# Padded buffers, S5 tables on GpSimd's queue and a last FFN on the unnormed residual, in a two-layer hybrid trunk

## The chip, the cores and the metric

The kernel runs on one core of a Trainium2 chip. The metric is the device time of one execution in microseconds, as the median of several runs. A core has TensorE for matmuls, VectorE and ScalarE for elementwise work, GpSimd for odd work, and SyncE, which here only issues DMAs. ScalarE and GpSimd have a DMA queue of their own as well.

## The reference

It is a trunk of two layers over 256 latent tokens and 256 context tokens of width 1024. Each layer is a half SwiGLU step, a mixer and another half SwiGLU step; every sublayer norms its input, shifts and scales it, and adds a gated result to the residual.

```
def ffn_half_step(h, m, k, g, w_gate, w_up, w_down):
    shift, scale, gate = m[:, :, 3 * k], m[:, :, 3 * k + 1], m[:, :, 3 * k + 2]
    hn = modulate(rmsnorm(h, g), shift, scale)          # rmsnorm(h, g) * (1 + scale) + shift
    return h + 0.5 * gate * swiglu(hn, w_gate, w_up, w_down)
...
for i in range(DEPTH):                                  # DEPTH = 2
    lat = ffn_half_step(lat, m_lat, 0, norm_ffn1[i], *ffn1)
    cx = ffn_half_step(cx, m_ctx, 0, norm_ffn1[i], *ffn1)
    # even: latent attention heads and S5 channel groups; odd: Hyena channels and RG-LRU channels
    y_ctx, y_lat = even_mixer(...) if i % 2 == 0 else odd_mixer(...)
    lat = lat + m_lat[:, :, 5] * y_lat
    lat = ffn_half_step(lat, m_lat, 2, norm_ffn2[i], *ffn2)
    if not last: cx = the same for the context
return rmsnorm(lat, final_norm)
```

The FFN's hidden width is 2816. The attention has 8 heads, the S5 part 32 groups of 16 channels with 64 complex states, scanned in both directions. The context drops out behind the odd mixer, so the last FFN and the final norm see the latent half alone.

## The kernel before

Everything lies transposed: 128 channels on the partitions, 512 tokens in the columns (context 0 to 255, latent 256 to 511). The residual `res` is a constant tile of 8 x 512. Matmuls run in float32r with operands split into a high and a low part: `mm3` issues three matmuls for each block of 128 channels (lines 158, 159 and 160; with one stream order kept, all three stand on line 155). A weight block comes in by `wload`: a DMA from SyncE's queue into one of four `raw` buffers (line 142), a cast on ScalarE (148) and a subtraction on VectorE (149) into one of four `w` buffers.

A tile framework places instructions and buffers: each engine runs its own list in order, a pool gives a tag so many buffers, and a request for a buffer waits until its last user is done. The constant pool `cst` comes first in memory, then `rawp`, `wp`, the small tiles `sm`, and then the pools of a stage, which `phase` opens in the order of its arguments.

- In the first stage the FFN runs while `s5_prepare` builds tables for eight passes of S5 and writes them to DRAM: `d_mb`, `d_g`, `d_v`, `d_e`.
- In the even mixer, `s5_states` loads the tables `mb` and `et` of a pass (lines 916 and 918) and `s5_out` loads `gm` (958) and, in eight pieces, `tz` from `d_v` (962), all from SyncE's queue. VectorE does the scan between the two (935 to 950). The store of a pass's result to `d_y` goes out from GpSimd (971). The passes are interleaved with keys and queries of four pairs of heads and then with the eight heads: scores (L848 to L866), transposed probabilities (881, 887), values (900). Keys get their rotary part by a DMA from GpSimd (774). GpSimd also does two small memsets a pass (942, 949).
- Between the odd mixer and the last FFN, `out_proj` (through `down`) adds each of eight residual tiles (429) and its squares (291, 292); then `norm_proj` takes the row statistics (253 to 278), norms each tile (309, 314, 316) and starts the matmuls.
- `final` does the same at the end: statistics, row broadcast, a multiply for each of eight tiles (1266) and a store of each (1269). The host transposes the result.

## Time and profile before

| | |
|---|---|
| median of 3 runs | 1797.6 us (1797.04 to 1797.97) |
| the profiled execution, its own time | 1795.22 us |
| its span, from the first instruction to the last end | 1793.4 us |
| mean granted TensorE clock | 0.986 of full speed |

A profile is of one execution. A line of it names an engine, the kernel's line, the operation, and "written <- read" tiles with their shapes. Busy time is the union of an engine's instructions; TensorE's matmuls overlap in the pipeline, so the distance from one start to the next is the pace, and the duration of one is longer.

### The profile page before, as it was taken

The page shows a single profiled execution, that of the slowest core. Times are in us where ns is not written, and L with a number is a line of the kernel's source. Part 1 is how long each engine was busy: PE and PEld are TensorE (multiplying, and loading weights), DVE is VectorE, ACT ScalarE, POOL GpSimd, SP SyncE. Part 2 cuts the span into 40 slices and gives each one's busy share as a digit, 9 for nine tenths or more (in the row PEclk, how much of TensorE's full clock was granted, in tenths as well). Part 3 has the DMA queues.
Part 4 walks back from the last instruction along what each step waited for, and adds up shares of the span by engine and source line. Part 5 has one row for each costly group of instructions (what it writes and reads, how often), then busy time and mean ns, then how long its engine had stood idle before and what let it go on. Part 6 is the DMA issues. An engine that isn't in the chain of part 4 may idle for free.

```text
span 1793.4 us, 24725 instructions
## 1 busy us (share of the span) xinstructions
PE 1727.7 (96%) x9364; PEld 1444.7 (81%) x9364; DVE 1252.9 (70%) x2464; ACT 684.1 (38%) x1082; POOL 13.2 (1%) x47
## 2 busy tenths in 40 slices
PE   5999999999989999999999999999999999789997
PEld 3778777779868788778888888888888888589997
DVE  7999999987488668776666686544543576875555
ACT  4433333343445653222222233222122357554442
POOL 0000000000000000000000000000000000000000
PEclk9999999999998999999999999999999999799999
DMA  9566666652465453464454544555433225146552
GB/s 324 173 216 211 223 214 216 210 189 90 125 185 172 120 189 115 154 223 152 147 183 153 164 130 130 179 173 163 156 117 95 94 94 201 49 150 191 183 185 92
DMA packets 108055, 292.63 MB, mean 163 GB/s; under 512 B 21216, under 2 KB 36448, under 8 KB 107680
## 3 DMA queue, kind: packets, MB, share of 16 engines
q1 hardware_dynamic: 102368, 287.39, 49.8%
q10 hardware_dynamic: 4928, 2.10, 0.7%
q8 instruction: 73, 1.20, 0.3%
q0 software_dynamic: 640, 1.57, 0.3%
q14 instruction: 46, 0.38, 0.1%
HBM read 272.20 MB, written 18.28 MB: 162 GB/s over the span
## 4 chain that ended last, share of the span: by engine, by line
PE 87%; DVE 7%; DMA 2%; ACT 1%; issue 1%; SPq 1%; DVEq 0%; ACTq 0%
PE mm L158 25%; PE mm L160 25%; PE mm L159 25%; PE mm L155 6%; DVE w L149 1%; DMA h<-in_modw_dram 1%; PE mm L1148 1%; SPq L981 1%; DVE nt L309 1%; DMA x<-d_g 1%; DVE x L316 1%; DMA x<-d_v 0%; PE ps L278 0%; PE ps L631 0%; PE ps L1059 0%
## 5 line engine op out<-in xcount | busy, mean ns | idle before, releaser
L159 PE MATMUL mm<-x,w 128*128 128x512 f32 (+1 forms) x1600 | 575.1, 360 | 0.0
L160 PE MATMUL mm<-x,w 128*128 128x512 f32 (+1 forms) x1600 | 574.5, 360 | 0.0
L158 PE MATMUL mm<-x,w 128*128 128x512 f32 (+1 forms) x1600 | 569.4, 361 | 4.5 <-ACT x L314 3.3
L148 ACT CAST w<-raw 128x1024 fp32r<-128x1024 f32 (+2 forms) x324 | 328.5, 1018 | 527.7 <-issue 254.1
L149 DVE TENSOR_TENSOR w<-raw,w 128x1024 fp32r<-128x1024 f32 (+2 forms) x324 | 384.0, 1187 | 191.7 <-ACT w L148 190.8
L158 PEld LDWEIGHTS mm<-x,w 128*128 128x128 f32 x1600 | 300.9, 189 | 55.9 <-ACT x L314 3.9
L159 PEld LDWEIGHTS mm<-x,w 128*128 128x128 f32 x1600 | 301.8, 189 | 48.9 <-issue 2.0
L160 PEld LDWEIGHTS mm<-x,w 128*128 128x128 f32 x1600 | 301.8, 189 | 48.7 <-issue 1.2
L225 DVE CUSTOM_DVE_ANT_0 junk<-m,sc 128x1024 f32<-128x1024 f32 x224 | 273.3, 1220 | 1.8 <-DMA m<-in_modw_dram 0.2
L158 PE MATMUL mm<-h,w 128*128 128x512 f32 (+1 forms) x632 | 229.2, 367 | 0.0
L160 PE MATMUL mm<-h,w 128*128 128x512 f32 (+1 forms) x632 | 228.4, 364 | 0.0
L159 PE MATMUL mm<-h,w 128*128 128x512 f32 (+1 forms) x632 | 228.3, 363 | 0.0
L429 DVE SCALAR_TENSOR_TENSOR res<-mm,mraw,res 128x256 f32<-128x256 f32 x192 | 86.1, 480 | 103.7 <-PE mm L160 92.8
L459 DVE TENSOR_TENSOR h<-h,mm 128x512 f32<-128x512 f32 (+1 forms) x88 | 54.6, 621 | 128.5 <-PE mm L160 111.0
L458 ACT ACTIVATE h<-mm 128x512 f32<-128x512 f32 (+1 forms) x88 | 48.0, 545 | 234.5 <-PE mm L160 223.7
L159 PEld LDWEIGHTS mm<-h,w 128*128 128x128 f32 x632 | 119.1, 188 | 20.6 <-issue 1.0
L158 PEld LDWEIGHTS mm<-h,w 128*128 128x128 f32 x632 | 118.6, 188 | 21.0 <-issue 1.1
L160 PEld LDWEIGHTS mm<-h,w 128*128 128x128 f32 x632 | 118.9, 188 | 20.5 <-issue 0.6
L155 PE MATMUL mm<-x,w 128*128 128x256 f32 x384 | 66.1, 289 | 6.7 <-DVE x L316 6.2
L314 ACT ACTIVATE x<-nt,mraw 128x256 fp32r<-128x256 f32 x88 | 42.9, 506 | 54.5 <-DVE nt L309 54.5
L155 PEld LDWEIGHTS mm<-x,w 128*128 128x128 f32 x384 | 53.9, 188 | 11.6 <-DVE x L316 9.2
L165 DVE TENSOR_TENSOR h<-h,h 128x512 fp32r<-128x512 f32 (+1 forms) x88 | 54.5, 619 | 0.0
(345 smaller groups left out, 1604.5 us busy)
## 6 DMA issues: line engine op xcount, KB each, us to landing
raw<-in_wgu_dram SPq DMA_DIRECT2D x176, 512.0 KB, 3.8
m<-in_modw_dram SPq DMA_DIRECT2D x130, 512.0 KB, 4.3
raw<-in_wd_dram SPq DMA_DIRECT2D x64, 512.0 KB, 3.6
raw<-in_wd_dram SPq DMA_DIRECT2D x32, 384.0 KB, 3.3
raw<-in_od_in_dram SPq DMA_DIRECT2D x20, 512.0 KB, 3.5
h<-in_modw_dram SPq DMA_DIRECT2D x12, 512.0 KB, 9.9
raw<-in_ev_in_dram SPq DMA_DIRECT2D x10, 512.0 KB, 3.5
d_mb<-mbt SPq DMA_DIRECT2D x16, 256.0 KB, 2.9
```

What stands on the lines that cost most here:

```text
L148: nc.scalar.copy(hi[:, :n], raw[:, :n])
L149: nc.vector.tensor_sub(lo[:, :n], raw[:, :n], hi[:, :n])
L155: mm = lambda *a, **k: self.keep(self.nc.tensor.matmul(*a, **k))
L158: mm(ps, lhsT=wh, rhs=xh, start=first and i == 0, stop=False)
L159: mm(ps, lhsT=wh, rhs=xl, start=False, stop=False)
L160: r = mm(ps, lhsT=wl, rhs=xh, start=False, stop=last and i == n - 1)
L165: self.nc.vector.tensor_sub(lo, src, hi)
L225: nc.vector.tensor_tensor_reduce(self.junk, w, self.sc[:, v, :], 1.0, 0.0, ALU.mult, ALU.add, raw[:, dt, v : v + 1])
L314: self.last_act = nc.scalar.activation(x[:, 0, c0:c1], y, AF.Identity, bias=b)
L429: self.nc.vector.scalar_tensor_tensor(r, ps[:, c0:c1], gate[:, i, VEC[h] : VEC[h] + 1], r, op0=ALU.mult, op1=ALU.add)
L458: nc.scalar.activation(s[:, 0, lo:hi], pg[:, lo:hi], AF.Silu)
L459: nc.vector.tensor_mul(s[:, 1, lo:hi], s[:, 0, lo:hi], pu[:, lo:hi])
```

## The change

- Two pads of 136 and 64 float32 a partition are put at the head of the constant and the small pool, and the first stage's pools are opened in another order (`x`, `h`, then the rest).
- In the first stage the kernel writes a fifth table, `d_z`, from `d_v`: the shifted pieces that `tz` needs, laid out as one block, by four DMAs a pass from GpSimd.
- In the even mixer `mb`, `et`, `gm` and `tz` (now one DMA from `d_z`) are loaded from GpSimd's queue. GpSimd's memsets and the rotary key copies go to VectorE, the store to `d_y` to ScalarE's queue. The scores of the first head are emitted with the first pair's keys and queries.
- The last FFN (`ffn_last`) no longer norms its input. While the odd mixer's `out_proj` finishes a residual tile, `unscaled` writes it times gain into the high and low parts, and puts the shift into two further columns. The matmuls run over 258 columns; the row norm `rb` is multiplied onto gate and up behind the matmul and the shift's product is added as a bias.
- In the last `down`, `final_tiles` multiplies each finished tile by the final gain and transposes it into four PSUM buffers; `final` scales those by the row statistics and stores them row by row, so that the host need not transpose.

```
+        for p, k in ((self.cst, 136), (self.sm, 64)):
+            p.tile([P, k], F32, tag="pad", name=f"pad{k}", bufs=1)
+        self.done = None
...
         if last:
             self.stat(i, h)
+            if self.done is not None:
+                self.done(i, h)
...
+    def ffn_last(self, l, k, xs):
+        nc, t = self.nc, self.t
+        idx = 2 * l + k // 2
+        n = NTOK
+        with self.tc.high_priority(offset=SOON):
+            rb = self.slot("g", [P, n])
+            nc.scalar.copy(rb, self.rstd([self.acc[LAT]], self.inv_d))
+        gate = self.need(l, 3 * k + 2)
+        for f0, f1 in CHUNKS:
+            hid = []
+            for f in range(f0, f1):
+                pg, pu = self.pm(), self.pm()
+                for g, ps in enumerate((pg, pu)):
+                    w = self.wload(t["wgu"][idx, f, g], D)
+                    self.mm3(ps[:, : n + 2], self.wparts(w, KT), self.parts(xs, 0, n + 2))
+                b = self.small([P, 2], "bias")
+                s = self.slot("g", [P, 2, n])
+                nc.vector.tensor_copy(b[:, 0:1], pg[:, n : n + 1])
+                nc.vector.tensor_mul(s[:, 0, :], pg[:, :n], rb)
+                nc.scalar.activation(s[:, 0, :], s[:, 0, :], AF.Silu, bias=b[:, 0:1])
+                nc.vector.tensor_copy(b[:, 1:2], pu[:, n : n + 1])
+                nc.vector.tensor_mul(s[:, 1, :], pu[:, :n], rb)
+                nc.vector.scalar_tensor_tensor(s[:, 1, :], s[:, 1, :], b[:, 1:2], s[:, 0, :], op0=ALU.add, op1=ALU.mult)
+                hd = self.slot("x", [P, 2, T2], F32R)
+                self.split(hd[:, 0, n:T2], hd[:, 1, n:T2], s[:, 1, :])
+                hid.append(hd)
+            if f1 == NF:
+                self.done = self.final_tiles()
+            self.down(lambda i: t["wd"][idx, i][:, f0 * P : f1 * P], hid, gate, [LAT], f1 == NF, f1 - f0)
+
+    def unscaled(self, l, k, xs):
+        nc = self.nc
+        sh, sc = self.mod[l, 3 * k], self.mod[l, 3 * k + 1]
+        def done(i, h):
+            x, r, g = xs[i], self.res[:, i, h[0] : h[1]], sc[:, i, 0:1]
+            with self.tc.high_priority(offset=SOON):
+                nc.scalar.activation(x[:, 0, :NTOK], r, AF.Copy, scale=g)
+                nc.vector.scalar_tensor_tensor(x[:, 1, :NTOK], r, g, x[:, 0, :NTOK], op0=ALU.mult, op1=ALU.subtract)
+        for i, x in enumerate(xs):
+            self.split(x[:, 0, NTOK : NTOK + 2], x[:, 1, NTOK : NTOK + 2], sh[:, i, 0:1].to_broadcast([P, 2]))
+        return done
...
         nc.sync.dma_start(self.d_v[q], vt)
+        dv = self.d_v[q]
+        for g in range(4):
+            nc.gpsimd.dma_start(
+                self.d_z[q][:, g, :].rearrange("(r c) m -> r c m", r=L),
+                bass.AP(dv.tensor, dv.offset + g * 32 * 240, [[16, L], [240, 16], [1, P]]),
+            )
...
-                nc.gpsimd.dma_start(k[64:96, h, :], st["kr"][64:96])
+                nc.vector.tensor_copy(k[64:96, h, :], st["kr"][64:96])
...
+            if p == 0:
+                pr0 = self.scores(qs[0][:, 0, :], ks[0][:, 0, :])
...
-        nc.sync.dma_start(mb, self.d_mb[q])
+        nc.gpsimd.dma_start(mb, self.d_mb[q])
...
-        nc.sync.dma_start(et, self.d_e[q].rearrange("p e g c -> p e (g c)"))
+        nc.gpsimd.dma_start(et, self.d_e[q].rearrange("p e g c -> p e (g c)"))
...
-        nc.gpsimd.memset(rz[:, :, 0:1], 0.0)
+        nc.vector.memset(rz[:, :, 0:1], 0.0)
...
-        nc.gpsimd.memset(hv[:, :, 0:1], 0.0)
+        nc.vector.memset(hv[:, :, 0:1], 0.0)
...
-        nc.sync.dma_start(gm, self.d_g[q])
+        nc.gpsimd.dma_start(gm, self.d_g[q])
         tz = self.slot("x", [P, 4, P])
-        dv = self.d_v[q].rearrange("(g c) m -> c g m", g=4)[0:16]
-        for r in range(L):
-            nc.sync.dma_start(tz[r * 16 : (r + 1) * 16], dv[:, :, r * 16 : r * 16 + P])
+        nc.gpsimd.dma_start(tz, self.d_z[q])
...
-        nc.gpsimd.dma_start(d_y[q * 4 : (q + 1) * 4].rearrange("g s c n -> (s c) g n"), ys)
+        nc.scalar.dma_start(d_y[q * 4 : (q + 1) * 4].rearrange("g s c n -> (s c) g n"), ys)
...
+        self.xl = [self.slot("hy", [P, 2, T2], F32R) for _ in range(KT)]
+        self.done = self.unscaled(1, 2, self.xl)
         self.out_proj("od_out", 1, os, [LAT])
+        self.done = None
+
+    def final_tiles(self):
+        nc = self.nc
+        self.fin = [[self.pm() for _ in range(2)] for _ in range(2)]
+        def done(i, h):
+            y = self.slot("g", [P, NTOK])
+            nc.scalar.activation(y, self.res[:, i, h[0] : h[1]], AF.Copy, scale=self.gain[:, 6, i : i + 1])
+            for j in range(2):
+                nc.tensor.transpose(self.fin[j][i // 4][:, i % 4 * P : (i % 4 + 1) * P], y[:, j * P : (j + 1) * P], self.ident)
+        return done
 
     def final(self):
         nc = self.nc
-        self.rb[LAT] = self.rstd([self.acc[LAT]], self.inv_d)
-        for i in range(KT):
-            y = self.slot("h", [P, NTOK])
-            nc.vector.scalar_tensor_tensor(
-                y, self.res[:, i, NTOK:T2], self.gain[:, 6, i : i + 1], self.rb[LAT], op0=ALU.mult, op1=ALU.mult
-            )
-            nc.sync.dma_start(self.out[i], y)
+        _, r = self.rstd_stats([self.acc[LAT]], self.inv_d)
+        for j in range(2):
+            for q in range(2):
+                y = self.slot("g", [P, T2])
+                if q:
+                    nc.scalar.activation(y, self.fin[j][q], AF.Copy, scale=r[:, j : j + 1])
+                else:
+                    nc.vector.tensor_scalar(y, self.fin[j][q], r[:, j : j + 1], None, op0=ALU.mult)
+                (nc.scalar if q else nc.sync).dma_start(self.out[j, :, q * T2 : (q + 1) * T2], y)
...
-        self.phase(x=8, **s5p, gs=2, sc=1, junk=1, m=2, ct=1, h=10)
+        self.phase(x=8, h=10, sc=1, junk=1, m=2, **s5p, gs=2, ct=1)
...
-        self.phase(x=8, h=10)
-        self.ffn(1, 2, [LAT])
+        self.ffn_last(1, 2, self.xl)
         self.final()
```

## Rows read from the trace of the kernel before

**Rows 1.** The page's first part: busy time, share of the span, instructions.

```profile
PE 1727.7 (96%) x9364; PEld 1444.7 (81%) x9364; DVE 1252.9 (70%) x2464; ACT 684.1 (38%) x1082; POOL 13.2 (1%) x47
```

**Rows 2.** Windows by stage: stretch, length, PE PEld DVE ACT POOL, clock, DMA, GB/s.

```profile
62.00:404.00 342.00, 341.52 (x1591) 270.68 (x1592) 317.22 (x595) 128.06 (x199) 1.01 (x9) 1.00 0.66 208
404.00:500.00 96.00, 94.31 (x573) 83.35 (x572) 57.51 (x171) 36.65 (x63) 4.33 (x10) 1.00 0.42 116
500.00:610.00 110.00, 101.39 (x620) 82.40 (x619) 91.50 (x178) 63.36 (x154) 6.67 (x19) 0.92 0.55 167
...
630.00:1480.00 850.00, 844.94 (x4069) 696.98 (x4068) 524.61 (x901) 259.46 (x365) 0.00 (x0) 1.00 0.46 148
1480.00:1520.00 40.00, 40.00 (x281) 34.73 (x280) 24.43 (x37) 29.17 (x44) 0.00 (x0) 1.00 0.58 200
...
1591.00:1782.00 191.00, 189.71 (x1584) 189.51 (x1584) 111.19 (x154) 85.35 (x125) 0.00 (x0) 0.99 0.51 160
```

**Rows 3.** Windows of two dense stretches, of 512 and of 256 columns.

```profile
1200.00:1300.00 100.00, 100.00 (x432) 81.08 (x431) 51.22 (x73) 24.46 (x29) 0.00 (x0) 1.00 0.50 158
1640.00:1700.00 60.00, 60.00 (x508) 60.00 (x507) 35.07 (x45) 27.60 (x38) 0.00 (x0) 1.00 0.61 194
```

**Rows 4.** The chain of work, odd mixer's plain fp32 matmuls: start, length, what.

```profile
1476.73 12.88 PE mm L1148 x30
```

**Rows 5.** TensorE's waits: total us, times, longest.

```profile
PE ps L966 <- DMA x<-d_v: 7.3, 1, 7.3
```

**Rows 6.** Timeline of SyncE's queue in the even mixer: start, length, line, operation.

```profile
523.02 8.32 SPq L142 DMA_DIRECT2D raw<-in_ev_out_dram  x3
531.44 0.38 SPq L958 DMA_DIRECT2D x<-d_g  x1
```

**Rows 7.** The chain of work behind that issue.

```profile
531.44 5.08 DMA x<-d_g
```

**Rows 8.** Window behind TensorE's wait.

```profile
545.00:562.00 17.00, 17.00 (x112) 14.55 (x112) 11.79 (x22) 9.18 (x22) 1.54 (x4) 0.84 0.53 155
```

**Rows 9.** Timeline of GpSimd: key copies and one store of a pass.

```profile
467.05 2.14 POOL L774 DMA_DIRECT2D q<-kr  x4 [86.65 <-issue]
561.45 0.75 POOL L971 DMA_DIRECT2D d_y<-ys  x1 [4.46 <-ACT ys L970]
```

**Rows 10.** DMA issues, 470 to 625 us: count, KB each, median us to landing.

```profile
d_y<-ys POOLq DMA_DIRECT2D x8, 128.0 KB, 2.7
```

**Rows 11.** VectorE's groups by form: count, busy us, mean ns, idle before.

```profile
L833 DVE TENSOR_TENSOR q<-q,nt 32x256 f32<-32x256 f32 x8 | 3.2, 415 | 0.2
L668 DVE MEMSET et<- 128x8 f32 x8 | 0.5, 65 | 0.1
```

**Rows 12.** Timeline of TensorE between the odd mixer and the last FFN.

```profile
1583.59 0.28 PE L160 MATMUL mm<-x,w 128*128 128x256 f32 x1
1586.68 0.58 PE L253 MATMUL ps<-inv_d,acc 128*128 128x1 f32 x4 [2.82 <-DVE acc L292]
...
1591.62 0.80 PE L158 MATMUL mm<-x,w 128*128 128x256 f32 x2 [1.11 <-ACT x L314]
```

**Rows 13.** VectorE's groups by form from 1591 us to the end.

```profile
L149 DVE TENSOR_TENSOR w<-raw,w 128x1024 fp32r<-128x1024 f32 x56 | 68.3, 1225 | 45.9 <-ACT w L148 45.9
L429 DVE SCALAR_TENSOR_TENSOR res<-mm,mraw,res 128x256 f32<-128x256 f32 x24 | 11.3, 481 | 16.4 <-PE mm L160 16.2
L459 DVE TENSOR_TENSOR h<-h,mm 128x256 f32<-128x256 f32 x22 | 9.3, 421 | 11.3 <-PE mm L160 6.0 <-ACT h L458 5.0 <-issue 0.3
L267 DVE SCALAR_TENSOR_TENSOR rs_a<-rs_y,rs_v 128x1 f32<-128x1 f32 x6 | 1.0, 215 | 0.0
```

**Rows 14.** Timeline of the end.

```profile
1785.57 0.76 PE L278 MATMUL ps<-ident,rs_y 128*128 128x128 f32 x4 [2.02 <-DVE rs_y L269]
1786.36 3.22 DVE L1266 SCALAR_TENSOR_TENSOR h<-res,gain,ps 128x256 f32<-128x256 f32 x8 [0.73 <-PE ps L278]
1786.87 3.78 SPq L1269 DMA_DIRECT2D out_dram<-h  x8
```

More of the change, by code (lines that the diff above doesn't have):

```diff
@@ L687, in s5_prepare @@
         self.d_v = dt("d_v", [P, 240])
+        self.d_z = dt("d_z", [P, 4, P])
         self.d_e = dt("d_e", [P, 2, 8, 64])
@@ L810, in even_mixer @@
             i = s5_begin()
-            pr = self.scores(qs[h // 2][:, h % 2, :], ks[h // 2][:, h % 2, :]) if h < H else None
+            pr = None
+            if h < H:
+                pr = self.scores(qs[h // 2][:, h % 2, :], ks[h // 2][:, h % 2, :]) if h else pr0
             s5_end(i)
@@ L1486 @@
         aps[name] = nc.dram_tensor(f"in_{name}_dram", a.shape, mybir.dt.from_np(a.dtype), kind="ExternalInput").ap()
-    out = nc.dram_tensor("out_0_dram", (KT, P, NTOK), F32, kind="ExternalOutput").ap()
+    out = nc.dram_tensor("out_0_dram", (2, P, D), F32, kind="ExternalOutput").ap()
     with tile.TileContext(nc, schedule_with_timeline_sim=True) as tc:
@@ L1491 @@
     got = r.results[0]["out_0_dram"]
-    return np.ascontiguousarray(got.reshape(D, NTOK).T).reshape(1, NTOK, D)
+    return np.ascontiguousarray(got).reshape(1, NTOK, D)
```

## The prediction

> **What bounds the kernel now.** I read first the busy table, then the span cut into stages with each engine's busy time, then the chain of work, the waits of TensorE, and last SyncE's and GpSimd's own queues in the even mixer. TensorE is busy 96% of the span, VectorE 70% [rows 1], but the stages differ [rows 2]: from 62 to 404 us TensorE is full and VectorE has 317 of 342 us; from 630 to 1480 and from 1591 to 1782 TensorE is full and VectorE has room; from 500 to 610 neither is full (TensorE 101, VectorE 91.5 of 110). So what counts is the pace of TensorE's stream nearly everywhere, and waits in a few places.
>
> The pace is worth a second look. In a dense 100 us there are 432 matmuls of 512 columns, 231.5 ns each, and in a dense 60 us 508 of 256 columns, 118.1 ns each [rows 3], at a granted clock of 1.00, the 2.4 GHz level. That is 556 and 283 cycles: the difference is 273 cycles for 256 columns, 1.066 a column, with about 10 cycles per instruction. The plain fp32 matmuls of the odd mixer (30 in 12.88 us [rows 4]) take 429.3 ns, 1030 cycles for 512 columns: 2 cycles a column and 6 over. They read at half the rate of the float32r ones and lose nothing. So the float32r stream loses some 7% to something that bites only at full reading rate.
>
> **The padding.** The pads add 544 bytes a partition behind the constants and 256 behind the small tiles; the new bias tile adds 4 x 32. Adding up the tiles of the kernel before (constants step in 32 bytes) the raw buffers begin at byte 37,344, the weights at 53,728, x at 97,376: each 32 bytes past a multiple of 64, and so all large buffers, h of the first stage among them. Afterwards raw begins at 37,888, the weights at 54,272 and x at 98,304, all multiples of 1,024, and h follows x directly because the first stage's pools change order. No float32r operand before lies on a multiple of 64, so no row shows that pace; it has to be bounded. From below the gain is nothing: the loss belongs to the float32r stream whatever its address. From above the whole loss goes: the fp32 rows' 6 cycles over give (512+6)/2.4 = 216 ns and 109 ns. A supposition with the right size can be made: if each piece of 64 bytes (16 columns) that straddles a boundary costs one cycle more, 512 columns take 544+6 cycles = 229 ns and 256 take 278 = 116 ns, within 3 ns of both measured paces, and it would stay hidden at half rate as in [rows 4]. Two shapes and the fp32 rows fit it, so I take the value near the upper end: 217 and 111 ns, a cut of 6.3% and 6.0%.
>
> [...]
>
> By stage [rows 2]: 62 to 404: 6.3% of 342 is 21.5 us, but TensorE would then need 320 us against VectorE's 317, so I take 15. 404 to 500: 5. 630 to 1480: 6.3% of 845 = 53. 1480 to 1520: 2. 1591 to 1782: 6.0% of 190 = 11. From 500 to 630 and 1520 to 1591, where VectorE or transfers set the pace, nothing. Sum 86 us.
>
> **The even mixer.** TensorE's longest wait of the stage is 7.3 us for the d_v table [rows 5]. It is no slow transfer: SyncE stood 8.32 us on ev_out weight loads whose buffers were not free, and only behind them issued d_g and the eight small d_v loads [rows 6]; d_g then landed in 5.08 us [rows 7]. Behind the hole the granted clock is 0.84 in the mean from 545 to 562 [rows 8], part of it at the 1.2 GHz level after TensorE had stood idle, worth at most 0.16 x 17 = 2.7 us. With all four tables on GpSimd's queue no weight load stands ahead of them, and d_z makes eight issues into one. The order on that queue is mb, et of a pass, then gm, tz of the pass before; each still waits for a free x buffer. GpSimd now carries one d_y store a pass, 0.75 us, and eight key copies, 0.53 us each [rows 9]; its memsets and these go away, so four loads of perhaps 0.75 to 1 us a pass come to 3 or 4 us of the 12 us that a pass takes (nine turns in the 110 us of [rows 2]). Its stores land in 2.7 us [rows 10]. The d_y store goes to ScalarE, behind the copy that makes it, and adds an issue there. The 32 d_z writes run in the first stage, where GpSimd does nothing else.
>
> The floor is VectorE: 91.5 us busy of 110 [rows 2]. It takes on eight key copies of 32x512 (0.4 each from the 32x256 row, 0.8 at most) and 16 memsets of 0.065 [rows 11], 4 to 7.5 us, about half of it before 500 where it has 38 us free [rows 2]; the first head's scores move ahead as well. So 110 can come down to about 97: between 3 and 16, I take 11 us saved.
>
> **The last FFN's entry.** The last od_out matmul starts at 1583.59; then come the sum of squares, the row statistics at 1586.68, and the first matmul of the new FFN at 1591.62 [rows 12], 8 us in which TensorE does nothing but the statistics' small matmuls. Now each finished residual tile is scaled by ScalarE and split by VectorE at once, and the norm is applied behind the matmul; seven of eight operands wait ready, and the eighth takes residual, copy and split, about three times 0.48 us [rows 13], under the first 21 matmuls, 2.5 us. Saved 7 to 9, I take 8. Cost: VectorE gets one more 128x256 split (0.48) per od_out tile, near its limit there; per hidden tile it has two multiplies, a scalar_tensor_tensor and a split (0.42, 0.42, 0.48, 0.42) and two one-column copies (0.2 at most) where it had a multiply and a split, 1.3 us more by [rows 13]. With two weight splits of 1.23 that is 4.6 us beside the 5.7 us of 48 matmuls: covered. 258 columns instead of 256 on 1,056 matmuls: 2/2.4 ns each, +1 us.
>
> **The end.** Before, row broadcast, eight multiplies of 3.22 us and eight stores issued from 1786.87 over 3.78 us [rows 14]. Now gains and 16 transposes run inside the down stream (at most 0.19 us each by the four of L278, up to 3 us; I take 2), and behind the statistics two scaled copies on each of two engines (0.5 to 1 us each) and two stores on each of two queues: the end comes 3 to 4 us earlier. Net 1 to 2 us saved; four of the six PSUM buffers are then held, and two remain for down, whose residual takes 0.48 us of a tile's 24 matmuls, 2.8 us. I take 2.
>
> **Sum.** 86 + 11 + 8 - 1 + 2 = 106. The profiled execution took 1795.2 us (span 1793.4 and 1.8 around it), 2.4 under the median of 1797.6. 1795.2 - 106 = 1689, on the median's scale 1691; I say 1690.
>
> **Rivals.** *The padding does nothing* (0.30). The loss per column belongs to float32r at full rate; the same 1.066 holds for x, h and q tiles, which speaks for neither. The remaining 20 us come alone: 1778, from 1768 to 1788. The Trainium skill (SBUF — State Buffer, "Door 1: The DMA port swizzle") counts 16-byte lines, of which a start 32 bytes on crosses no more, and this rival follows from it; its "Operand start alignment" says that it timed nothing. No row here decides.
>
> *No change to be measured* (0.04): the padding is idle, and VectorE's extra work in the mixer and at the od_out tail takes back the 20 us: 1797.
>
> *GpSimd's queue becomes the bound* (0.07): its four loads a pass take so long to issue that a pass waits for them. A pass takes some 12 us, so it decides from 3 us a load. At 4 us, 16 us a pass, eight passes lose 32 us; with an idle padding and the 9 us of the last FFN and end: 1797.6 + 32 - 9 = 1821. Against it stand 0.75 us an issue and 2.7 us to landing in a stretch where VectorE is over 80% busy [rows 9, 10]. The Trainium skill (SBUF — State Buffer, "SBUF: two separate sides", the box on SWDGE) has VectorE's two-port operations lock GpSimd out of writing descriptors; these rows show no such delay so far.
>
> *Padding pays, the rest as said* (0.59): 1690, its own range 1670 to 1712 (all of the loss and a VectorE that keeps up in the first stage, or half of the first stage's and no gain in the mixer).
>
> The 80% range takes in the first and the last of these: 1670 to 1786. By 0.2% either side (3.6 us, about what a measurement of this kernel tells from no change): faster 0.89, same 0.04, slower 0.07.
>
> **What would show it.** Dense stretches of float32r matmuls at 216 to 218 ns and 110 to 111 ns; if they stay at 231 and 118 the padding is idle and the time is near 1778. No wait of TensorE on d_v or d_z above 2 us, and GpSimd issues under 1 us. No gap above 1 us between od_out and the last FFN, and an end within 4 us of the last statistics. VectorE above 95% from 62 to 404 us would show that the first stage gave less than 15.

## The result and the profile after

The kernel after takes 1775.8 us (median of 4 runs, 1775.09 to 1776.01), the kernel before beside it 1797.3 (1796.6 to 1797.97): ratio 0.988, 95% interval 0.9863 to 0.9897. The change makes the kernel 21.5 us faster, where 1690 us and a cut of 106 were forecast. The time lies inside the range, close to the rival in which the padding does nothing (1778), but not for that rival's reason: a change of pace by itself gave 22 us (e6), and the rest of the change nothing on balance.

The first part of the page after: busy time, share of the span (1773.2 us), instructions, as in [rows 1].

```profile
PE 1708.4 (96%) x9376; PEld 1444.4 (81%) x9376; DVE 1271.4 (72%) x2570; ACT 696.5 (39%) x1103; POOL 37.4 (2%) x79
```

Windows of the kernel after by stage, columns as in [rows 2]:

```profile
62.00:396.00 334.00, 333.29 (x1586) 269.17 (x1587) 314.67 (x593) 126.55 (x198) 19.79 (x39) 1.00 0.70 220
396.00:500.00 104.00, 98.27 (x584) 87.43 (x583) 60.64 (x178) 39.53 (x67) 2.71 (x5) 0.97 0.36 116
500.00:610.00 110.00, 101.18 (x626) 79.52 (x624) 94.32 (x200) 66.52 (x158) 14.54 (x27) 0.95 0.49 158
630.00:1460.00 830.00, 824.99 (x4055) 692.42 (x4054) 520.89 (x898) 256.31 (x360) 0.00 (x0) 1.00 0.47 151
1460.00:1500.00 40.00, 40.00 (x279) 34.61 (x278) 24.33 (x37) 29.09 (x44) 0.00 (x0) 1.00 0.60 198
1564.00:1764.00 200.00, 195.91 (x1611) 194.85 (x1609) 132.59 (x248) 91.69 (x129) 0.00 (x0) 0.99 0.51 161
```

The stretch from 630 us, 850 us long before, now takes 830; that from 500 still takes 110, with TensorE as busy as before. The last FFN, from its first matmul to its last residual tile, takes 9 us more than before, and TensorE, full before, misses 4 us in it.

The two dense stretches, to be held against [rows 3]:

```profile
1200.00:1300.00 100.00, 100.00 (x443) 82.81 (x442) 52.65 (x76) 23.97 (x28) 0.00 (x0) 1.00 0.52 165
1640.00:1700.00 60.00, 60.00 (x502) 60.00 (x501) 40.57 (x69) 27.23 (x34) 0.00 (x0) 1.00 0.58 182
```

At 512 columns 443 matmuls fit into 100 us: 225.7 ns where there were 231.5, and not 217. The shorter ones (now 258 columns in some 310 of 502, and 256 in the rest) take 119.5 ns where 256 took 118.1: slower, not 111. The fill of a window is coarse, as it counts matmuls that reach over an edge, so from here on a pace is the mean distance from one start to the next. For 512 columns of `x` tiles, over the whole kernel and without gaps above 300 ns, it is 232.5 ns before and 227.1 after.

To see where the time went I cut every trace at the ends of VectorE's 192 residual additions (number 48, 64, 160, 168, 176, 184, 192). All lengths are in us and from one execution each; e2, e3, e6 and e7 are experiments below.

| stage | before | after | e3 pads | e6 shift | e2 no pads | e7 no pads, new order |
|---|---|---|---|---|---|---|
| first stage | 428.0 | 420.1 | 420.6 | 423.6 | 422.5 | 419.8 |
| even mixer with its output projection | 248.3 | 252.2 | 251.7 | 247.5 | 245.3 | 252.1 |
| the FFNs between the mixers | 762.8 | 746.8 | 746.8 | 746.8 | 746.8 | 746.9 |
| odd mixer with its output projection | 145.2 | 146.0 | 144.8 | 144.9 | 145.5 | 146.1 |
| last FFN: entry and first 8 tiles | 60.9 | 53.3 | 62.6 | 63.2 | 56.9 | 53.7 |
| its second 8 tiles | 68.3 | 69.0 | 68.9 | 68.3 | 69.3 | 68.5 |
| its last 8 tiles | 68.4 | 76.2 | 69.1 | 69.1 | 76.2 | 76.2 |
| from there to the end | 11.6 | 9.7 | 12.2 | 12.1 | 9.9 | 9.9 |

From before to after: first stage -7.9, FFNs between -16.0, entry -7.6 and end -1.9, but even mixer +3.9, odd mixer +0.7 and the last 16 tiles +8.5.

TensorE's waits of the kernel after from 414 to 675 us: total, times, longest.

```profile
PE mm L913 <- DVE q L898: 5.8, 1, 5.8
PE mm L159 <- DVE x L320: 2.8, 3, 1.3
PE mm L159 <- ACT x L318: 1.9, 1, 1.9
PE mm L946 <- DVE p L929: 1.7, 1, 1.7
```

The 7.3 us for d_v [rows 5] are gone, and no wait for d_z has come. In their place stand 5.8 us for the rotated queries of the first head, whose scores were emitted early, and at the mixer's entry 4 us for the norm's tiles. GpSimd's queue does what was said of it (start, length, line):

```profile
508.48 0.53 POOL L981 DMA_DIRECT2D x<-d_mb  x1 [3.52 <-DVE x L1001]
509.00 0.53 POOL L983 DMA_DIRECT2D x<-d_e  x1
520.30 0.53 POOL L1023 DMA_DIRECT2D x<-d_g  x1 [10.78 <-issue]
522.51 0.55 POOL L1025 DMA_DIRECT2D x<-d_z  x1 [1.69 <-DVE sm_st L925]
```

The entry of the last FFN, against [rows 12]; the last matmul of the odd mixer and the first of the FFN:

```profile
1564.29 0.28 PE L164 MATMUL mm<-x,w 128*128 128x256 f32 x1
1564.40 0.28 PE L162 MATMUL mm<-hy,w 128*128 128x258 f32 x1
```

The hole of 8 us is closed. In the last eight tiles, however, TensorE's transposes show (timeline, then the window around the first):

```profile
1738.38 0.44 PE L1336 MATMUL mm<-ident,g 128*128 128x128 f32 x2 [1.90 <-ACT g L1334]
...
1753.71 0.44 PE L1336 MATMUL mm<-ident,g 128*128 128x128 f32 x2 [1.27 <-ACT g L1334]
...
1764.48 0.44 PE L1336 MATMUL mm<-ident,g 128*128 128x128 f32 x2 [1.26 <-ACT g L1334]
```

```profile
1736.00:1744.00 8.00, 6.11 (x37) 5.90 (x38) 2.19 (x3) 2.50 (x4) 0.00 (x0) 0.79 0.22 66
```

TensorE stands three times, 4.4 us in all, for a tile that ScalarE scales; behind the first wait the clock is 0.79 in the mean, and that tile takes 6.7 us where others take 2.9. At the end (against [rows 14]) the scaled copies start at 1767.26, the stores are issued at 1768.04 and the span ends at 1773.2:

```profile
1767.26 1.40 DVE L1349 TENSOR_SCALAR g<-mm,rs_y 128x512 f32<-128x512 f32 x2
...
1768.04 1.00 SPq L1350 DMA_DIRECT2D out_dram<-g  x2
```

### The profile page after: what moved, and what is told of

The parts are those of the page before. It is cut to its first block, busy times and chain, and to the rows that moved or that the text cites. A ratio compares the mean times of both kernels' runs of the same rounds, so it can differ in the third digit from the quotient of the medians.

```text
span 1773.2 us, 24766 instructions
## 1 busy us (share of the span) xinstructions
PE 1708.4 (96%) x9376; PEld 1444.4 (81%) x9376; DVE 1271.4 (72%) x2570; ACT 696.5 (39%) x1103; POOL 37.4 (2%) x79
## 5 line engine op out<-in xcount | busy, mean ns | idle before, releaser
L163 PE MATMUL mm<-x,w 128*128 128x512 f32 (+1 forms) x1424 | 521.0, 366 | 0.1
L164 PE MATMUL mm<-x,w 128*128 128x512 f32 (+1 forms) x1424 | 520.2, 366 | 0.0
L162 PE MATMUL mm<-x,w 128*128 128x512 f32 (+1 forms) x1424 | 516.3, 368 | 3.5 <-ACT x L318 2.2
L162 PEld LDWEIGHTS mm<-x,w 128*128 128x128 f32 x1424 | 268.3, 189 | 50.4 <-issue 2.8
L163 PEld LDWEIGHTS mm<-x,w 128*128 128x128 f32 x1424 | 269.3, 189 | 44.4 <-issue 2.0
L164 PEld LDWEIGHTS mm<-x,w 128*128 128x128 f32 x1424 | 269.3, 189 | 43.4 <-issue 1.2
L162 PE MATMUL mm<-h,w 128*128 128x512 f32 x456 | 178.3, 394 | 0.0
L164 PE MATMUL mm<-h,w 128*128 128x512 f32 x456 | 176.9, 390 | 0.0
L163 PE MATMUL mm<-h,w 128*128 128x512 f32 x456 | 176.7, 390 | 0.0
L465 DVE TENSOR_TENSOR h<-h,mm 128x512 f32<-128x512 f32 x66 | 45.3, 686 | 107.2 <-PE mm L164 95.0
L464 ACT ACTIVATE h<-mm 128x512 f32<-128x512 f32 x66 | 39.4, 597 | 195.4 <-PE mm L164 184.7
L162 PEld LDWEIGHTS mm<-h,w 128*128 128x128 f32 x456 | 85.6, 188 | 19.0 <-issue 1.1
L163 PEld LDWEIGHTS mm<-h,w 128*128 128x128 f32 x456 | 85.6, 188 | 18.4 <-issue 1.0
L164 PEld LDWEIGHTS mm<-h,w 128*128 128x128 f32 x456 | 85.6, 188 | 18.3 <-issue 0.6
L163 PE MATMUL mm<-hy,w 128*128 128x258 f32 x352 | 99.7, 284 | 0.0
L164 PE MATMUL mm<-hy,w 128*128 128x258 f32 x352 | 99.7, 283 | 0.0
L162 PE MATMUL mm<-hy,w 128*128 128x258 f32 x352 | 99.3, 283 | 0.0
```

The source lines that it names most:

```text
L162: mm(ps, lhsT=wh, rhs=xh, start=first and i == 0, stop=False)
L163: mm(ps, lhsT=wh, rhs=xl, start=False, stop=False)
L164: r = mm(ps, lhsT=wl, rhs=xh, start=False, stop=last and i == n - 1)
L464: nc.scalar.activation(s[:, 0, lo:hi], pg[:, lo:hi], AF.Silu)
L465: nc.vector.tensor_mul(s[:, 1, lo:hi], s[:, 0, lo:hi], pu[:, lo:hi])
```

## Experiments

The kernel before, timed beside them, had medians from 1796.3 to 1798.5 us; ratios are to it, with 95% intervals. Where the intervals of two runs overlap, as for e2 and e7, e10 or e8, or for e11 and e12, their difference is read from the stages of one execution each.

### e1: a map of the pace by address

A kernel that leaves the whole trunk out and runs groups of 24 matmuls:

```
for o, k in run(96, 480, 512):        # x offset, weight offset (bytes past a multiple of 1024), columns
    tc.keep_in_program_order(mm(o, **k))     # for each block: (wh, xh), (wh, xl), (wl, xh)
```

> This kernel leaves the whole trunk out. It runs only groups of 24 float32r matmuls of the mm3 kind (512, 256 and 258 columns) from one x and one weight buffer, each group at its own byte offset of the two against a multiple of 1024, and at the end some groups again beside elementwise work of ScalarE and VectorE or beside loads. What is read is the distance from one start to the next in each group. Theory A (the address sets the pace, as in the padding step of the prediction, but for less than was said): groups at offsets (x 96, weights 480), those of the kernel before, run at about 232 ns for 512 columns, the group at (0, 0) at 227, and a scan of one offset alone shows at which multiple the pace jumps; for 256 columns 118 to 120 at any address. Theory B (the address is idle; the other engines' traffic or the order of the stream sets the pace): all groups of 512 columns run within 1 ns of one another, and the groups beside elementwise work or loads run slower than the quiet ones. Theory C (the prediction's own supposition, hidden behind something else in the trunk): quiet groups at (0, 0) run at 216 to 217 and 109 to 111 ns, those at 32 past a multiple of 64 at 229 to 232 and 116 to 118.

Measured, mean distance of starts in ns, second round of the quiet groups:

| x offset, weight offset | 512 columns | | x offset, weight offset | 512 columns |
|---|---|---|---|---|
| 96, 480 (as before) | 232.4 | | 0, 32 | 233.1 |
| 0, 0 | 227.8 | | 0, 256 | 228.3 |
| 32, 0 | 232.7 | | 0, 512 | 226.7 |
| 128, 0 | 233.5 | | 32, 32 | 227.8 |
| 256, 0 | 227.3 | | 96, 96 | 227.8 |
| 512, 0 | 226.7 | | 32, 64 | 233.3 |
| 64, 0 | 228.7 | | 4, 0 | 238.0 |

Beside elementwise work or loads the groups at (0, 0) took 226.7 to 228.3 and those at (96, 480) 232.3 to 233.1 ns, so other engines' traffic made no difference. Theory A's numbers hold: both paces of the trunk come out, and the address sets them, but not by alignment: (32, 32) and (96, 96), on no multiple of 64, are as fast as (0, 0), and (128, 0) as slow as (32, 0). What the fast groups share is that x and the weights stand at the same place modulo 256. Nothing of 512 columns ran at 217, so theory C is out. Groups of 256 columns took 116.8 to 119.9 ns.

### e2 and e3: the pads taken away, the pads alone

e2 is the kernel after without the pads and with the old pool order:

```
-        for p, k in ((self.cst, 136), (self.sm, 64)):
-            p.tile([P, k], F32, tag="pad", name=f"pad{k}", bufs=1)
...
-        self.phase(x=8, h=10, sc=1, junk=1, m=2, **s5p, gs=2, ct=1)
+        self.phase(x=8, **s5p, gs=2, sc=1, junk=1, m=2, ct=1, h=10)
```

> The kernel after without the two pads and with the first stage's pools in their old order; all else as after. Theory A (the address gives the 24 us that the first-stage, middle and last-but-one FFN stages gained): about 1798 to 1801, pace of 512 columns back at 231 to 233 ns. Theory B (the address is idle, and the stages gained by other parts of the change): 1776 within 3, pace still at 227 ns.

e3 is the kernel before with the reverse of this edit (96 in place of 64, as it has no bias tile).

> The kernel before with only the two pads (sized for the same addresses as after) and the new pool order. Theory A (the address sets the pace of 512 columns, 232.5 against 227 ns): some 24 us faster, 1771 to 1775, which is at or below the kernel after, as the rest of the change then nets nothing. Theory B (address idle): 1797 within 3. Theory C (the prediction's 217 ns, lost by another part of the change): 1712.

Measured: e2 1773.5 us, ratio 0.9859 (0.9843 to 0.9876), pace 227.1 ns: theory A is out by 25 us, and theory B has the time and the pace, though the address is not idle (e1). e3 1779.2, 0.9899 (0.9882 to 0.9916), pace 227.2: theory A's pace, but 4 us over its time, which the new pool order adds in the even mixer (251.7 against 247.5 in e6, below). The pads bring the pace to the kernel before and are worth nothing in the kernel after. The distances, added up from the tiles as in the prediction, solve it. Before, x lies 97,376 - 53,728 = 43,648 bytes above the weights, 128 past a multiple of 256. The new bias tile of the last FFN puts 128 bytes between the two, so without pads it is 43,776, which is 171 times 256; with pads 44,032, 172 times 256. The bias tile had already done by accident what the pads were for.

### e5 and e6: the distance of two operands, and 32 floats

e5 is a second map, by the distance d of x from the weights.

> As the first map, the whole trunk is left out; groups of 24 matmuls, now by the distance d of the x operand from the weight operand in steps of 32 bytes up to 224, at 512, 256 and 258 columns, with both operands moved together in some groups; then groups with one and the same weights, with plain fp32, and with the weights kept for two matmuls in a row. Theory A (from the first map: the pace hangs on the distance of the two operands modulo 256 bytes, not on where either lies): d = 0 at 227 ns for 512 columns, d = 64 near 229, all others 232 to 234, and the same with both moved by 128; at 256 columns d = 0 at 120 and the others 117 to 119. Theory B (absolute places matter as well): groups moved together differ by over 2 ns from those that stand at the same distance. For the 10 ns between 227 and the 217 of the prediction: if the weight load takes them, one and the same weights or weights kept for two matmuls run faster than 227, near 217; if it is the stream's own, they stay at 227.

Windows of e5, one for each group of 24 matmuls (length / 24 is the pace; the counts include instructions that reach over an edge). In order: 512 columns at d = 0, 32, 64, 128, 192, at 64 and 192 with both operands moved by 128; 256 columns at d = 0, 128, 192, and 192 with both moved by 480; 128 and 384 columns at d = 0; 512 with one and the same weights.

```profile
150.70:156.17 5.47, 5.47 (x27) 4.51 (x26) 0.16 (x1) 0.00 (x0) 0.00 (x0) 1.00 0.00 0
156.17:161.77 5.60, 5.60 (x26) 4.50 (x24) 0.16 (x1) 0.00 (x0) 0.00 (x0) 1.00 0.00 0
161.77:167.27 5.50, 5.50 (x25) 4.51 (x24) 0.16 (x1) 0.00 (x0) 0.00 (x0) 1.00 0.00 0
172.88:178.48 5.60, 5.60 (x25) 4.50 (x24) 0.16 (x1) 0.00 (x0) 0.00 (x0) 1.00 0.02 3
184.10:189.71 5.61, 5.61 (x26) 4.50 (x25) 0.16 (x1) 0.00 (x0) 0.00 (x0) 1.00 0.00 0
217.94:223.44 5.50, 5.50 (x26) 4.51 (x25) 0.16 (x1) 0.00 (x0) 0.00 (x0) 1.00 0.00 0
234.65:240.24 5.59, 5.59 (x25) 4.51 (x24) 0.16 (x1) 0.00 (x0) 0.00 (x0) 1.00 0.00 0
195.30:198.18 2.88, 2.88 (x26) 2.88 (x24) 0.16 (x1) 0.00 (x0) 0.00 (x0) 1.00 0.00 0
206.71:209.56 2.85, 2.85 (x27) 2.85 (x25) 0.16 (x1) 0.00 (x0) 0.00 (x0) 1.00 0.00 0
212.38:215.10 2.72, 2.72 (x26) 2.72 (x25) 0.16 (x1) 0.00 (x0) 0.00 (x0) 1.00 0.00 0
251.62:254.45 2.83, 2.83 (x26) 2.83 (x25) 0.16 (x1) 0.00 (x0) 0.00 (x0) 1.00 0.00 0
273.10:275.73 2.63, 2.63 (x26) 2.63 (x25) 0.16 (x1) 0.00 (x0) 0.00 (x0) 1.00 0.02 6
268.90:273.10 4.20, 4.20 (x27) 4.20 (x25) 0.16 (x1) 0.00 (x0) 0.00 (x0) 1.00 0.00 0
342.89:348.35 5.46, 5.46 (x25) 4.50 (x24) 0.16 (x1) 0.00 (x0) 0.00 (x0) 1.00 0.00 0
```

For 512 columns theory A holds: 227.8 ns at d = 0, 229.4 at 64, 233 to 235 elsewhere, and the same with both operands moved. For 256 columns the order turns round: 119.9 at d = 0, 116.6 to 119.6 at nearly all others; and there the absolute place counts too (theory B), 113.7 against 117.8 at the same d = 192.

The first distances of a group are uneven. In the last twelve of each, every group of 512 columns at d = 0, here and in e1, runs at 226.7 ns, as the kernel after does from 1200 to 1300 us; 384, 256 and 128 columns at d = 0 run at 173.3, 120.0 and 111.7. At 2.4 GHz that is 544, 416, 288 and 268 cycles: from 256 to 512 columns one cycle a column and 32 over, and 128 columns above that line. No address took away the 32 at 512 columns.

One and the same weights change nothing (5.46 us). Neither do weights kept for two matmuls in a row: 226.7 ns at d = 0 once the group is under way (one distance of 419 ns behind the plain fp32 group lifts its mean to 236.8), 233.5 at d = 32. But each matmul still has its weight load (24 in the third column), so these groups don't tell whether the load is those 32 cycles.

e6 uses the theory on the kernel before, with one line:

```
+        self.sm.tile([P, 32], F32, tag="pad", name="pad32", bufs=1)
```

> The kernel before with one pad of 32 float32 (128 bytes) in the small pool and nothing else: x and h move from 96 to 224 past a multiple of 256, where the weights already stand; nothing becomes a multiple of 64. Theory A (the distance of the two operands modulo 256 sets the pace of 512 columns): 227 ns, and without the new pool order's stall at the even mixer's entry 1770 to 1776. Theory B (alignment to a multiple of 64 or more sets it): pace at 231 to 233 and 1797.

Measured: 1775.1 us, 0.9871 (0.9855 to 0.9888). Theory A holds. 128 bytes in the kernel before are worth as much as the whole change. Dense stretches of e6, against [rows 3]:

```profile
1200.00:1300.00 100.00, 100.00 (x443) 82.81 (x442) 52.61 (x75) 23.98 (x28) 0.00 (x0) 1.00 0.53 168
1640.00:1700.00 60.00, 60.00 (x503) 60.00 (x502) 34.30 (x42) 25.14 (x34) 0.00 (x0) 1.00 0.59 183
```

### e7: the pool order alone

e2 with the new order of the first stage's pools and no pads.

> The kernel after without pads, with the first stage's pools in the new order. Theory A (the new order costs the even mixer its entry: the norm's tiles come to lie on buffers that are released late, 6 to 7 us): 1778 to 1781 against 1773.5 for the same with the old order, with the two waits of 1.85 and 1.3 us at 420 to 424 us back. Theory B (the pads and not the order bring that stall): 1773 to 1775.

Measured: 1776.2 us, 0.9878 (0.9863 to 0.9893). The even mixer goes from 245.3 to 252.1 us, the value of the kernel after. Windows of 16 us from the mixer's start, e7 and then e2:

```profile
420.00:436.00 16.00, 12.51 (x75) 11.69 (x76) 10.74 (x35) 5.06 (x12) 0.00 (x0) 0.79 0.26 91
```

```profile
423.00:439.00 16.00, 14.33 (x103) 12.95 (x102) 13.21 (x43) 6.30 (x13) 0.00 (x0) 1.00 0.10 35
```

In the same 16 us TensorE starts 75 matmuls and not 103, with a granted clock of 0.79, part of it at the 1.2 GHz level behind the waits for the norm's tiles. Theory A holds for the stage; in the kernel before, too, the order costs it 4.2 us (e3 against e6). The total moves by 2.7 us only and lies between the two theories, as the first stage and the last FFN's entry came out 2.7 and 3.2 us shorter in e7; e2 has a wait of 2.3 us there, for a multiply with the row norm, that e7 lacks. What brings that wait, no run shows.

### e4, e8, e9: the parts of the even mixer

e4 is the kernel after with the first head's scores emitted in the head loop as before.

> The kernel after, with the first head's scores emitted in the head loop as in the kernel before. Theory A (the early scores put TensorE's 5.83 us wait for the rotated queries at the head of its queue, and with the half clock behind it they are why the even mixer got 4 us longer instead of 11 shorter): 4 to 7 us faster, 1769 to 1772, and no wait of TensorE above 2 us at the first scores. Theory B (the wait only moves: TensorE would find nothing else to do while VectorE is behind): 1776 within 2, with a wait of similar length a little later. Theory C (the early scores are a gain that something else hides): 3 to 6 us slower.

Measured: 1777.5, 0.9887 (0.9871 to 0.9902). Theory B: the wait moved to the first head's transposes.

```profile
PE mm L942 <- DVE p L925: 5.7, 1, 5.7
```

e8 is e2 with the eight key copies on GpSimd's DMAs:

```
-                nc.vector.tensor_copy(k[64:96, h, :], st["kr"][64:96])
+                nc.gpsimd.dma_start(k[64:96, h, :], st["kr"][64:96])
```

> The kernel after without pads, with the keys' rotary part copied by GpSimd's DMAs as before and no longer by VectorE. Theory A (VectorE is the bound from the first scan to the last, 89.9 us for what took 85.5 before, and the eight copies of 0.42 us are most of it): 2 to 4 us faster than 1773.5. Theory B (GpSimd's queue, which now carries the tables, delays keys or tables): 2 us or more slower. Theory C (nothing on the path): within 1.

Measured: 1770.5, 0.9851 (0.9837 to 0.9866), theory A's time, but the even mixer takes 245.5 us, as without the edit. The 3 us are the last FFN's entry, 53.1 us, near that of e7. For the mixer it is theory C.

e9 is e2 with the four loads of a pass on SyncE's queue (`nc.sync.dma_start` in each).

> The kernel after without pads, with the four S5 loads of a pass on SyncE's queue again; the one-block table d_z is kept. Theory A (TensorE is busy some 234 us of the even mixer in every kernel so far and idle some 12 to 13, before as after, so a wait that is removed comes back elsewhere): within 3 us of 1773.5, with TensorE's idle time in the even mixer between 11 and 15 us although waits on tables come back. Theory B (the tables' queue is worth the 7.3 us of the wait for d_v): 7 us or more slower, 1780 or over.

Measured: 1779.5, 0.9906 (0.9891 to 0.9921), even mixer 253.8 us, 8.5 longer; theory A falls, and theory B is missed by half a microsecond. TensorE's waits in e9:

```profile
PE mm L949 <- ACT p L928: 7.4, 2, 7.3
PE ps L989 <- DVE q L895: 4.7, 1, 4.7
PE ps L1026 <- DMA x<-d_z: 2.6, 2, 1.8
```

So, with the rest of the change there, GpSimd's queue is worth 8.5 us. Yet the whole mixer of the change gives 2.2 at the same pace (e6 247.5, e2 245.3).

### e13 and e15: the tables alone

e13 is e6 with `mb`, `et`, `gm` and, from d_z, `tz` on GpSimd's queue, and nothing else of the change.

> The kernel before with the 32-float pad, and of the change's even mixer only the tables: mb, et, gm and, in one block from d_z, tz on GpSimd's queue. Keys, memsets and the d_y store stay with GpSimd, the first head's scores stay late. Theory A (the wait for d_v is gone and with it some 7 us; the other edits of the mixer take it back): even mixer 238 to 242 us against 247.5, total 1766 to 1770. Theory B (the wait moves to the next thing that is late, the softmax and the scan behind VectorE): even mixer 245 to 248, total 1773 to 1776. Theory C (GpSimd's queue holds the tables behind key copies and stores): even mixer over 250.

Measured: 1782.1, 0.9914 (0.9898 to 0.9931); even mixer 253.6 us, longer than with the wait for d_v: theory C's number. First and last S5 scan of e13 and then of e6, whose mixers begin at 421.4 and 423.6 us:

```profile
499.16 1.22 DVE L953 TENSOR_TENSOR_SCAN x<-x,x 128x512 f32<-128x512 f32 x1
...
582.57 1.22 DVE L953 TENSOR_TENSOR_SCAN x<-x,x 128x512 f32<-128x512 f32 x1
```

```profile
507.76 1.22 DVE L945 TENSOR_TENSOR_SCAN x<-x,x 128x512 f32<-128x512 f32 x1
...
593.82 1.22 DVE L945 TENSOR_TENSOR_SCAN x<-x,x 128x512 f32<-128x512 f32 x1
```

The last scan starts 161.2 and not 170.2 us into the stage: the tables do come sooner. But the heads fall behind: the first head's scores start at 100.6 and not 92.6 us into the stage, the last head's at 174.5 and not 168.5. Their softmax needs the same VectorE as the scans, which would fit. Theory C's queue is not ruled out: the last two key copies leave it at 506.7 us, behind tables, and not by 485.2 as in e6, though TensorE shows no wait for keys. No run separates the two. ScalarE, behind them, changes its activation table five times from 589 to 610 us, as GELUs of S5 come between the exponentials.

e15 issues the four GELUs behind the last exponential:

```
+            with self.tc.issue_after(self.last_exp.ins):
                 nc.scalar.activation(y, y, AF.Gelu_apprx_tanh)
```

> The kernel before with the 32-float pad and the tables alone on GpSimd's queue, with the four GELUs of S5 issued behind the last exponential of the last head. Theory A (the GELUs among the exponentials cost the tail its time: three table loads of 1.28 us and the softmax of the last heads behind them): even mixer 246 to 250 us against 253.6, total 1774 to 1779 against 1782. Theory B (the attention is late because S5's scans now go ahead of its softmax on VectorE; the table loads lie beside that): within 1.5 us of 253.6.

Table loads of ScalarE from 580 to 625 us, e13 and then e15:

```profile
L993 ACT ACT_TABLE_LOAD x3 | 3.8, 1283 | 0.3 <-issue 0.3
...
L866 ACT ACT_TABLE_LOAD x2 | 2.6, 1283 | 0.0
...
L1011 ACT ACT_TABLE_LOAD x1 | 1.3, 1283 | 0.0
```

```profile
L994 ACT ACT_TABLE_LOAD x1 | 1.3, 1283 | 0.0
...
L1012 ACT ACT_TABLE_LOAD x1 | 1.3, 1283 | 0.0
```

Measured: 1780.0, 0.9921 (0.9898 to 0.9945); even mixer 251.2. The GELUs among the exponentials cost 2.4 of the 6 us, between the two theories; the last head's scores still come late, at 175.5.

### e10, e11, e12, e14, e16: the end, and the fastest

e10 is e2 with the old end.

> The kernel after without pads, with the old end: no gains and transposes inside the last down stream, and statistics, row broadcast, eight multiplies and eight stores behind it. Theory A (the transposes in the stream cost 7 us, the new end gives 2 back): 4 to 6 us faster than 1773.5, the last eight residual tiles in 69 us and not 76. Theory B (the last stretch is longer for another reason, such as the 120 ns pace or the last FFN's own work): within 1 of 1773.5.

Measured: 1768.7, 0.9845 (0.983 to 0.986), last eight tiles 69.4 us and not 76.2, end 11.6 and not 9.9: theory A.

e11 keeps the new end, with each tile's transposes issued two tiles late, and takes e8's key copies.

```
+            self.late.append((i, y))
+            if len(self.late) > 2:
+                self.turn()               # the two transposes of the oldest tile
```

> The kernel after without pads, with the keys' copies on GpSimd's DMA and the last transposes issued two tiles late, so that TensorE finds the scaled tile ready. Theory A (TensorE waited for ScalarE's scaled tile, and four of six PSUM buffers held cost nothing): the last eight residual tiles in 69 to 70 us, the end still in 10: 1763 to 1766. Theory B (the two PSUM buffers left are the limit): 73 us or more for these tiles, 1768 to 1771.

Measured: 1763.7, 0.9816 (0.98 to 0.9833), last eight tiles 70.6 us, end 9.9: theory A, and two PSUM buffers are enough. The last wait for a tile:

```profile
PE mm L1342 <- ACT g L1332: 1.0, 1, 1.0
```

e12 adds 64 bytes ahead of the last stage's pools.

> The kernel of the run before with 16 float32 of padding at the head of the last stage's pools, so that its x and hy operands lie 64 bytes past the weights modulo 256 and not at 0. Theory A (the map holds in the trunk: at distance 64, 118.0 ns for 256 columns where distance 0 takes 119.9, and 118.6 where 258 columns take 121.0): 1056 matmuls save 2.4 ns and some 900 save 1.9, together 4 us faster than the run before. Theory B (in the trunk the stream of 256 columns is set by something else): within 1.

Measured: 1761.6, 0.9803 (0.9789 to 0.9818). Neither theory: the last FFN takes 192.4 us and not 193.0. 256 columns follow the map, 117.8 ns where e11 has 119.9, as they did before (118.7 at a distance of 128, 118.7 in the map). 258 columns do not: 121.3 where e11 has 120.6, and their 1,056 matmuls take back most of the gain. The map had 258 columns at one place of the weights only.

e14 takes the early scores out of e12, and e16 gives e12 the late GELUs of e15.

> The fastest kernel so far (no pads but 16 float32 in the last stage, keys' copies on GpSimd's DMA, transposes two tiles late) with the first head's scores emitted in the head loop as before. Theory A (the early scores stop TensorE's queue for 2.8 to 5.8 us and give nothing back): 2 to 4 us faster than 1761.6, even mixer 241 to 243. Theory B (the wait moves to the first head's transposes, as it did with the keys on VectorE): within 1.5 us, even mixer 244 to 246.

> The fastest kernel so far with the same delay of the GELUs. Theory A: even mixer 241 to 243.5 us against 244.9, total 1758 to 1760. Theory B: within 1 us of 1761.6.

Measured: e14 1763.7, 0.9807 (0.9792 to 0.9822), even mixer 246.5: near theory B, half a microsecond past both its bounds, and far from theory A. e16 1759.7, 0.9801 (0.9785 to 0.9818), even mixer 243.6 us (244.9 in e12), theory A's time and the lowest median here; its interval overlaps that of e12, so its gain is not shown. It beats both kernels.

## Why the prediction was wrong

**Padding, -86: the step that failed.** The supposition that pieces of 64 bytes straddle a boundary fitted two paces and had the wrong cause. Aligned to 1,024, the stream runs at 227.1 ns, not 217, and 256 columns at 120, not 111. What counts at 512 columns is the distance of x from the weights modulo 256 (e1, e5, e6): -2.3%, not -6.3%. That the time came to lie near the 1778 of an idle padding is luck: a pace worth 22 us (e6) stands there in place of the 20 us forecast for the rest, which came to nothing on balance. The stretch priced at 53 us gave 16.0, the first stage 4.4 to 7.9 for 15, and the last FFN lost some 3 us by the pace alone (e6) where 11 were to be gained. Splitting a pace into "1.066 a column and 10 cycles" from two shapes was the slip: three shapes at d = 0 give one cycle a column and 32 fixed. And the upper bound came from the fixed part of plain fp32 matmuls, which the float32r stream never showed. At 256 columns the records of weight loads fill the stretch entirely [rows 3], and 128 columns still take 111.7 ns (e5), so the 111 ns forecast for 256 lie below what half as many columns take. The Trainium skill (TensorE: Matmul & The Clock Gate, "LDWEIGHTS (loading the stationary operand)") puts a load at its columns over 1.2 in ns, by which 128 columns take 106.7 ns, an estimate; the 111.7 ns lie 5 above it, and the trace's own records of a load are 192 ns long there and overlap.

**Even mixer, -11: measured +3.9.** The wait for d_v did go, and the queue issued as forecast. Two things were missed. The new pool order, booked under the padding, delays the norm's tiles: +6.9 us (e7). And the removed wait was hardly a gain. In all kernels TensorE's work in this stage, taken at full clock, is 228 to 231 us. The rest is idle time and half-clock time: before, 12.8 idle and 11.8 at half clock, which cost another 5.9. So 11 was over half of all there was. The kernel after has 15.4 idle and 12.1 at half clock. At equal pace the change's mixer gives 2.2 (e6 to e2): idle 12.4 to 12.8, at half clock 14.6 to 5.4. The tables alone lose 6 (e13): idle 13.9, at half clock 21.5, which is 1.5 and 3.5 of those us. That the earlier scans push the softmax back is argued, not shown. The price of VectorE's key copies was no part of it (e8). How the rest of the change turns e13's 253.6 into 245.3 was not taken apart edit by edit: early scores alone gain 0.6 and 1.6 us of the stage (e4, e14), key copies nothing, and the memsets and the store to `d_y` were not tried alone.

**Entry of the last FFN, -8: measured -7.6.** Right, its mechanism too; at equal pace (against e6's 63.2) it is -9.9, or -6.3 with the wait that e2 has there.

**258 columns, +1: right.** 120.6 against 119.9 ns in e11, times 1,056, is 0.7 us; by e5's 121.0 and 119.9 it is 1.2.

**End, -2: measured +5.9** (last eight tiles +7.8, rest -1.9). Of the 7.8, the transposes make 6.8 (e2 against e10) and the pace most of the rest (69.1 in e6). The rest was right; "transposes up to 3 us, I take 2" was wrong in kind: the cost is not their length but that TensorE's queue stops for ScalarE's tile, and then runs at half clock. Issued two tiles later they cost 1.1 us (e11 against e10). The stores' part was wrong by some 2 us too: from the last statistics to the end are 6.0 us, not 4.

**GpSimd's queue as the bound:** no issue over 0.77 us, no wait of TensorE for d_z. **VectorE in the first stage** reached 94% and TensorE stayed full, so it set no limit.

## What to carry to other kernels

When a pace is a few per cent off, move one operand against the other by 32 to 128 bytes before aligning anything, and measure it on the shape that fills the time: what helps 512 columns can hurt 256. Fit a cost per column only through three shapes at least, at the same addresses, and leave the first distances of a short group out. A removed wait can come back elsewhere; bound its worth by TensorE's own work in the stage, and put an instruction that depends on another engine some tiles behind its producer in TensorE's queue.

## What the runs showed of the hardware

A float32r matmul of 512 columns takes 226.7 ns in a steady stream when its moving operand lies a multiple of 256 bytes from its weights (e1, e5, the kernel after). It takes 228.9 at 64 bytes more, 232 to 234 at 16 bytes and at the other multiples of 32 tried, and 238 at 4 bytes. At the same distance modulo 256 the place of the two changed it by 1.6 ns at most, and work of ScalarE and VectorE or loads beside it by no more. Plain fp32 took 429.2 ns (e5). Why the distance counts, no run shows.

A wait of 1.9 and one of 1.4 us close together were followed by some 7 us at the 1.2 GHz level (e7's window). A lone wait had no fixed consequence: that of 1.9 us in the last eight tiles was followed by 3.4 us at this level, and one of 1.7 us in the even mixer by 3.4 us of it in e7 (from 547.9 us) and by none in the kernel after.
